# FFN in two phases, gate and up by seven products on two token chunks: a change to a hybrid encoder layer on one Trainium2 core

## The chip, the cores and the metric

The kernel runs on one core of a Trainium2 chip. The core has a matrix engine (TensorE, PE in the profile), a vector engine (VectorE, DVE), a scalar engine (ScalarE, ACT), GpSimd (POOL) and SyncE (SP), which work side by side and wait for each other by semaphores. SP and POOL also hold queues of transfers between DRAM and the on-chip memory. The metric is the device time of one run in microseconds (us).

## The reference

One layer of an encoder works on 1152 tokens (9 tiles of 128, or three chunks of 384) of 1024 features. The change is all in its last part, the FFN, and in the steps around it:

```
h   = x + w_out(sigmoid(gate_a) * (o_att @ w_att_out) + sigmoid(gate_s) * (y_ssd @ w_ssd_out))
hf  = rmsnorm(h, g_ffn)
out = h + (silu(hf @ w_gate) * (hf @ w_up)) @ w_down
y   = rmsnorm(out, g_final)
```

`w_gate` and `w_up` are 1024 x 2816, `w_down` is 2816 x 1024. All is in fp32.

## The kernel before

A product of two fp32 matrices is made of three matmuls. Each operand is split into a high part (a cast on ACT, line 126) and a low part (value minus high part, on DVE, line 127), and the high by high, high by low and low by high products are added in PSUM (`mm3`, lines 150 to 152). Weights come from DRAM in pieces of 512 KB (`wraw`, three buffers), are split into `whi` and `wlo` (three buffers each), and serve PE from there.

The FFN follows `w_out` and its norm. The `w_out` loop adds each product `ps_h` to `h` on DVE (line 897). `norm_T` then makes the normed tiles: a Square with a sum on ACT (line 162), the root on DVE and POOL (lines 119 and 121), the scaling `hn` on DVE (line 164), eight transposes per tile on PE into two banks `ps_T` (line 168), and their split into the chunk's `T_h`. Chunks 0 and 1 are normed within the last quarter of `w_out`, chunk 2 after it.

The FFN loop takes two tiles of 128 features (f) at a time, 11 pairs in all. For each of the two and for each of three token chunks it makes a gate and an up product, 24 matmuls of 384 columns each, then silu by Tanh (line 918) and two DVE operations (lines 919 and 921), and splits the result `a` into `ah` and `al`, which stay on chip. Then the down product of the pair follows: nine token tiles, two halves of 512 output columns, six matmuls into a bank `ps_d`, and one DVE add of that bank into `h` (line 931), 198 adds in the program. When all pairs are done, a tile's `h` is normed (Square on ACT, line 938, root, `yt` on DVE, line 940) and stored.

A scheduler sets the order of each engine's instructions ahead of the run from priorities, and the engines work through their queues in that order. Each queue is served in order, so an instruction that waits holds back all behind it. Transfers are issued by SP in order as well, and a load whose buffer isn't free holds back the loads behind it.

Ahead of `w_out`, the attention output `o_d` is read back from DRAM in five pieces through one buffer `oc` (line 815), split into `ohl` on ACT and DVE, and multiplied (`ps_ao`, from line 834).

Of the kernel before, what the change touches and what calls it, by code (L numbers as in the profile page):

```python
# [15 lines left out]
P = 128  # L16
D = 1024
# [25 lines left out]
def hybrid_layer_kernel(ctx: ExitStack, tc: tile.TileContext, x_prompt, x_sample, cache_k, cache_v,  # L43
# [20 lines left out]
    tpool = ctx.enter_context(tc.tile_pool(name="tpool", bufs=NC))  # L64
# [13 lines left out]
    bias_d = dram.tile([8, CH, 256], F32, name="bias_d")  # L78

# [105 lines left out]
    def run(gen):  # L185
        for _ in gen:
            pass
# [618 lines left out]
    hp = ctx.enter_context(tc.tile_pool(name="hp", bufs=1))  # L806
    with ExitStack() as ph:
        mp = ph.enter_context(tc.tile_pool(name="mp", bufs=1))
        m = mp.tile([P, KT, T], F32, name="m")
        ohl = hp.tile([P, 2, 4, T], F32R, tag="oh", name="ohl")  # L810
        ohi, olo = ohl[:, 0], ohl[:, 1]
        for t0 in range(0, T, 256):
            w = min(256, T - t0)
# [4 lines left out]
            for j in range(4):  # L818
                split(ohi[:, j, t0:t0 + w].rearrange("p (a w) -> p a w", w=qw),
                      olo[:, j, t0:t0 + w].rearrange("p (a w) -> p a w", w=qw), ov[:, :, j, :])  # L820

        for k in range(0, KT, 2):
# [7 lines left out]
            for kk in range(2):  # L830
                for c in range(NC):
# [5 lines left out]
                    mm3(ps[:, :CW], [(hi[:, j, cc], lo[:, j, cc], ohi[:, j, cs], olo[:, j, cs]) for j in range(4)])  # L837
# [33 lines left out]

    with ExitStack() as ph:
        h = hp.tile([P, NT, D], F32, tag="oh", name="h")
        psum_pools(ph, t=5)
        for t in range(NT):
            ld(out=h[:, t, :], in_=xrows(t))
        with ExitStack() as ph2:
            hnp = ph2.enter_context(tc.tile_pool(name="hnp2", bufs=4))
            gB = hnp.tile([P, D], F32, name="gB2", bufs=1)
            ld(out=gB, in_=g_ffn[0].partition_broadcast(P))  # L880
            fT = []
            for q in range(4):
# [7 lines left out]
                for t in range(NT):  # L890
# [5 lines left out]
                    hs = h[:, t, q * 256:(q + 1) * 256]  # L896
                    vec.tensor_tensor(out=hs, in0=ps[:, :256], in1=hs, op=ALU.add)
                    if q == 3 and t in (3, 6):
                        fT.append(norm_T(len(fT), lambda t: h[:, t, :], gB, hnp, "h"))
            fT += [norm_T(c, lambda t: h[:, t, :], gB, hnp, "h") for c in range(len(fT), NC)]  # L900

        with ExitStack() as ph2:
            fp = ph2.enter_context(tc.tile_pool(name="fp", bufs=2))
            for f0 in range(0, NF, 2):
                ah = fp.tile([P, 2, T], F32R, tag="ah", name=f"ah{f0}")
                al = fp.tile([P, 2, T], F32R, tag="al", name=f"al{f0}")
                for ff in range(2):
                    f = f0 + ff
                    gh, gl = wcols(w_gate[0], f * P, P, f"wfg{f}")
                    uh, ul = wcols(w_up[0], f * P, P, f"wfu{f}")  # L910
                    for c in range(NC):
                        cs = slice(c * CW, (c + 1) * CW)
# [89 lines left out]
```

## Time and profile before

| what | before |
|---|---|
| median of three runs | 1833.37 us (1833.11 to 1834.25) |
| the profiled execution | 1832.23 us, span 1830.4 us |
| PE busy | 1809.0 us, 99% |
| DVE busy | 920.9 us, 50% |
| ACT busy | 508.8 us, 28% |
| POOL busy | 113.1 us, 6% |
| DMA | 163.66 MB moved, 89 GB/s over the span |
| share of PE in the chain that ended last | 96% |

The span is the time from the first to the last event of the profiled execution; 1.83 us lie around it. Busy shares are averages over the whole program. Waits of PE are listed apart by what ended them. In the timeline a row's first two numbers are its start and its length in us; matmuls overlap, so the pace is the distance between two starts, not the length. A number in square brackets at the end of a row is the idle time just before it and what ended that.

### The profile page before, as it was taken

What the parts mean: (1) busy time and instruction counts of PE and PEld (TensorE: products, weight loads), DVE (VectorE), ACT (ScalarE), POOL (GpSimd) and SP (SyncE); (2) the same over time, 40 slices, a digit from 0 to 9 for tenths busy, and PEclk for the clock granted to TensorE, in tenths of its full rate; (3) what the DMA queues carried; (4) which work ended last, traced back from release to release, by engine and by line L of the source; (5) the groups of instructions that cost most, each with busy time, mean ns of one, the idle gap of its engine ahead of it and who ended that gap; (6) DMA issues with size and microseconds to landing.
All of it is one profiled execution on the core that took longest, in us unless ns stands there. A gap on an engine that the chain in (4) does not pass through costs nothing.

```text
span 1830.4 us, 26014 instructions
## 1 busy us (share of the span) xinstructions
PE 1809.0 (99%) x10767; PEld 1704.0 (93%) x10767; DVE 920.9 (50%) x1675; ACT 508.8 (28%) x989; POOL 113.1 (6%) x191
## 2 busy tenths in 40 slices
PE   7999999999999999999999999999999999999998
PEld 6998888999999999999999999989989899898997
DVE  5337777454998853533517343343442433424436
ACT  5235555422433323300305111111112111111112
POOL 1010000111121112000001000000000000000001
PEclk9999999999999999999999999999999999999999
DMA  7412212644755435653111111111101111111112
GB/s 217 82 56 66 66 58 70 202 153 132 222 187 180 147 94 184 209 199 98 59 32 47 47 35 35 47 46 47 47 24 47 47 47 47 27 50 40 47 35 103
DMA packets 193841, 163.66 MB, mean 89 GB/s; under 512 B 17507, under 2 KB 178503, under 8 KB 193580
## 3 DMA queue, kind: packets, MB, share of 16 engines
q1 hardware_dynamic: 183308, 128.54, 23.8%
q0 software_dynamic: 10416, 33.47, 4.7%
q8 instruction: 84, 1.38, 0.3%
q14 instruction: 33, 0.27, 0.0%
HBM read 123.21 MB, written 39.69 MB: 89 GB/s over the span
## 4 chain that ended last, share of the span: by engine, by line
PE 96%; DMA 2%; DVE 1%; ACT 1%; issue 0%; SPq 0%; POOL 0%; POOLq 0%; ACTq 0%
PE ps_mm L150 12%; PE ps_mm L152 11%; PE ps_mm L151 11%; PE ps_d L152 5%; PE ps_d L151 5%; PE ps_d L150 5%; PE ps_g L152 5%; PE ps_g L151 5%; PE ps_g L150 5%; PE ps_u L152 5%; PE ps_u L150 5%; PE ps_u L151 5%; PE ps_h L152 2%; PE ps_h L150 2%; PE ps_h L151 2%; DMA yc<-y_d 1%
## 5 line engine op out<-in xcount | busy, mean ns | idle before, releaser
L931 DVE TENSOR_TENSOR h<-ps_d,h 128x512 f32<-128x512 f32 x198 | 135.9, 691 | 121.8 <-PE ps_d L152 121.8
L150 PE MATMUL ps_g<-T_h,wfg_h 128*128 128x384 f32 x528 | 176.6, 334 | 0.0
L152 PE MATMUL ps_g<-T_h,wfg_l 128*128 128x384 f32 x528 | 176.6, 334 | 0.0
L151 PE MATMUL ps_g<-T_h,wfg_h 128*128 128x384 f32 x528 | 176.6, 334 | 0.0
L151 PE MATMUL ps_u<-T_h,wfu_h 128*128 128x384 f32 x528 | 176.4, 334 | 0.0
L152 PE MATMUL ps_u<-T_h,wfu_l 128*128 128x384 f32 x528 | 176.4, 334 | 0.0
L150 PE MATMUL ps_u<-T_h,wfu_h 128*128 128x384 f32 x528 | 176.4, 334 | 0.0
L151 PE MATMUL ps_d<-wd_l,ah 128*128 128x512 f32 x396 | 156.7, 396 | 0.0
L152 PE MATMUL ps_d<-wd_h,al 128*128 128x512 f32 x396 | 156.6, 395 | 0.0
L150 PE MATMUL ps_d<-wd_h,ah 128*128 128x512 f32 x396 | 153.0, 395 | 0.0
L921 DVE SCALAR_TENSOR_TENSOR fa<-ft,ps_u 128x384 f32<-128x384 f32 x66 | 36.6, 555 | 182.2 <-PE ps_u L152 182.2
L150 PE MATMUL ps_mm<-T_x,wx_h 128*128 128x384 f32 x288 | 100.1, 347 | 0.0
L150 PEld LDWEIGHTS ps_g<-T_h,wfg_h 128*128 128x128 f32 x528 | 99.1, 188 | 0.9
L151 PEld LDWEIGHTS ps_g<-T_h,wfg_h 128*128 128x128 f32 x528 | 99.1, 188 | 0.5
L152 PEld LDWEIGHTS ps_g<-T_h,wfg_l 128*128 128x128 f32 x528 | 99.1, 188 | 0.4
L126 ACT ACTIVATE wfu_h<-wfu_r 128x1024 fp32r<-128x1024 f32 x22 | 23.3, 1061 | 273.9 <-PE ps_d L152 240.8
L152 PEld LDWEIGHTS ps_u<-T_h,wfu_l 128*128 128x128 f32 x528 | 99.1, 188 | 0.0
L151 PEld LDWEIGHTS ps_u<-T_h,wfu_h 128*128 128x128 f32 x528 | 99.1, 188 | 0.0
L150 PEld LDWEIGHTS ps_u<-T_h,wfu_h 128*128 128x128 f32 x528 | 99.1, 188 | 0.0
L152 PE MATMUL ps_mm<-T_x,wx_l 128*128 128x384 f32 x288 | 97.4, 338 | 0.0
L151 PE MATMUL ps_mm<-T_x,wx_h 128*128 128x384 f32 x288 | 97.1, 337 | 0.0
L121 POOL TENSOR_TENSOR rs_r<-rs_v,mhalf 128x1 f32<-128x1 f32 x36 | 24.5, 683 | 1124.6 <-DVE rs_v L119 1124.6
(335 smaller groups left out, 4231.3 us busy)
## 6 DMA issues: line engine op xcount, KB each, us to landing
wfg_r<-in_w_gate_dram SPq DMA_DIRECT2D x22, 512.0 KB, 3.7
wfu_r<-in_w_up_dram SPq DMA_DIRECT2D x22, 512.0 KB, 3.9
wd_r<-in_w_down_dram SPq DMA_DIRECT2D x22, 512.0 KB, 4.1
acB<-ac_d SPq DMA_DIRECT2D x9, 1024.0 KB, 6.9
xbc_d<-cv POOLq DMA_DIRECT2D x36, 192.0 KB, 2.1
xb<-xbc_d SPq DMA_DIRECT2D x9, 768.0 KB, 6.1
wx_r<-in_w_in_dram SPq DMA_DIRECT2D x12, 512.0 KB, 4.5
z_d<-z POOLq DMA_DIRECT2D x24, 192.0 KB, 3.4
```

The costliest lines, as they stand in the source:

```text
L121: gps.tensor_tensor(out=r, in0=v, in1=mhalf[:, :n], op=ALU.pow)
L126: act.activation(hi, src, AF.Copy)
L150: pe.matmul(out, ah, bh, start=(i == 0), stop=False)
L151: pe.matmul(out, ah, bl, start=False, stop=False)
L152: pe.matmul(out, al, bh, start=False, stop=(i == n - 1))
L921: vec.scalar_tensor_tensor(out=a, in0=t, scalar=0.5, in1=pu[:, :CW], op0=ALU.mult, op1=ALU.mult)
L931: vec.tensor_tensor(out=h[:, t, hs], in0=ps, in1=h[:, t, hs], op=ALU.add)
```

## The change

The FFN becomes two phases. In the first, all gate and up products are made and `a` is stored to a DRAM tensor `a_d`, by a queue of POOL. In the second, the down product reads `a` and `w_down`, and adds over all 22 feature tiles in PSUM, so that nothing is added on DVE but once per bank at the end.

Gate and up on chunks 0 and 1 use a form with seven products for two by two blocks. The blocks are the two halves of the 1024 input features, the two feature tiles of a pair, and the two chunks. Each product is 12 matmuls of 384 columns (4 slices x 3). Sums of weight blocks (S1 to S4) are made on DVE in `prep`, sums of the activations (T1 to T4) once in `combine`, from raw fp32 copies of the transposed tiles. Products that share a destination are added in PSUM (banks `ps_a`, `ps_b`, `ps_c`), the rest by five DVE adds of 128x384 in `tail`. Chunk 2 goes by the plain form (`plain`, bank `ps_c2`).

In the second phase the token tiles go in two groups, of 5 and of 4, each through two halves of output columns, so `w_down` is read twice. `h` is stored to DRAM in the norm and read back as `y` in the second phase. At the end the last three pairs of the last half are run tile by tile. `o_d` is read in six pieces (256 and 128 columns of each chunk) rather than five.

On PE, at the end of `w_out`. `ps_h` is the product of `w_out`, `ps_T` the transposes, `hn_h` a normed tile (before, `hn_h_9733` and `hn_h_9755` are tiles 6 and 7; after, the three are tiles 6, 7 and 8), `ps_g` or `ps_a` the first gate product. Before:

```order
L151 MATMUL ps_h<-wo_l,T_m_8578 128x256
L152 MATMUL ps_h<-wo_h,T_m_8578 128x256
L168 MATMUL ps_T<-cp,hn_h_9733 128x128 x8
L150 MATMUL ps_g<-T_h_9468,wfg_h 128x384
L151 MATMUL ps_g<-T_h_9468,wfg_h 128x384
L152 MATMUL ps_g<-T_h_9468,wfg_l 128x384
```

Before, 40 gate and up matmuls further on:

```order
L152 MATMUL ps_u<-T_h_9468,wfu_l 128x384
L150 MATMUL ps_u<-T_h_9468,wfu_h 128x384
L168 MATMUL ps_T<-cp,hn_h_9755 128x128 x8
L151 MATMUL ps_u<-T_h_9468,wfu_h 128x384
L152 MATMUL ps_u<-T_h_9468,wfu_l 128x384
```

After:

```order
L155 MATMUL ps_h<-wo_h,T_m_8592 128x256
L913 MATMUL ps_T<-cp,hn_h_9765 128x128 x8
L913 MATMUL ps_T<-cp,hn_h_9788 128x128 x8
L913 MATMUL ps_T<-cp,hn_h_9811 128x128 x8
L881 MATMUL ps_a<-T_h_9489,wfg_h 128x384
L882 MATMUL ps_a<-T_h_9489,wfg_h 128x384
```

The transposes of the last two tiles moved from among the first gate and up matmuls to ahead of all of them.

On DVE at the same place. Before, from the last add of `ps_h` (`hn_h_9755` and `hn_h_9777` are tiles 7 and 8):

```order
L897 TENSOR_TENSOR h<-ps_h,h 128x256
L119 TENSOR_SCALAR rs_v<-ss 128x1
L127 TENSOR_TENSOR wfg_l<-wfg_r,wfg_h 128x1024
L164 SCALAR_TENSOR_TENSOR hn_h_9755<-h,rs_r,gB_8612 128x1024
L127 TENSOR_TENSOR T_h_9732<-ps_T,T_h_9732 128x4x128 x2
L119 TENSOR_SCALAR rs_v<-ss 128x1
L919 SCALAR_TENSOR_TENSOR ft<-ft,ps_g 128x384
L164 SCALAR_TENSOR_TENSOR hn_h_9777<-h,rs_r,gB_8612 128x1024
```

After, from the last add of `ps_h` (`raw` are the fp32 copies, `T_X` holds T1 and T2):

```order
L951 TENSOR_TENSOR h_8612<-ps_h,h_8612 128x256
L925 TENSOR_TENSOR raw_8633<-raw_8634,raw_8633 128x1536
L908 SCALAR_TENSOR_TENSOR hn_h_9788<-h_8612,rs_r,gB_8631 128x1024
L130 TENSOR_TENSOR wfu_l<-wfu_r,wfu_h 128x1024
L925 TENSOR_TENSOR raw_8634<-raw_8634 128x1536
L122 TENSOR_SCALAR rs_v<-ss 128x1
L130 TENSOR_TENSOR T_X<-raw_8633,T_X 128x1536
L130 TENSOR_TENSOR T_h_9764<-ps_T,T_h_9764 128x4x128 x4
L908 SCALAR_TENSOR_TENSOR hn_h_9811<-h_8612,rs_r,gB_8631 128x1024
```

Three operations of `combine` now stand between the last add and the norm of the last tile, and four splits of transposed tiles.

On ACT, where the first phase ends (`wd_0_4_h` is the high part of the third piece of `w_down`, whose buffer the last weights of up hold until the last but one matmul of the phase; `a_0` is the first piece of `a` read back, which the first down matmul needs). After:

```order
L1060 ACTIVATE fsg<-ps_c_13782 128x384
L1024 ACTIVATE p_13823<-ps_a 128x384
L129 ACTIVATE wd_0_2_h<-wd_0_2_r 128x1024
L129 ACTIVATE wd_0_4_h<-wd_0_4_r 128x1024
L129 ACTIVATE a_0_13988<-ar_0_14010 128x1280
L129 ACTIVATE a_2_13989<-ar_2_14050 128x1280
```

Before there is no such place: `a` is split from where DVE left it, pair by pair, and no load stands in front of it.

The diff, cut to its core (`prep`, `plain` and the views of arrays are left out where the words above say the same):

```diff
-        ohl = hp.tile([P, 2, 4, T], F32R, tag="oh", name="ohl")
-        for t0 in range(0, T, 256):
-            w = min(256, T - t0)
+        ohl = [hp.tile([P, 2, 4, CW], F32R, tag="oh", name=f"ohl{c}") for c in range(NC)]
+        for t0, w in ((c * CW + o, w) for c in range(NC) for o, w in ((0, 256), (256, 128))):
...
+            def combine(T1, T2, T3, T4):
+                b11, b21 = raws[0][:, :4, :], raws[0][:, 4:, :]
+                b12, b22 = raws[1][:, :4, :], raws[1][:, 4:, :]
+                sub = lambda out, a, b: vec.tensor_tensor(out=out, in0=a, in1=b, op=ALU.subtract)
+                sub(b11, b12, b11)
+                split(T1[:, 0], T1[:, 1], b11)
+                yield
+                sub(b11, b22, b11)
+                split(T2[:, 0], T2[:, 1], b11)
+                sub(b12, b22, b12)
+                split(T3[:, 0], T3[:, 1], b12)
+                sub(b21, b21, b11)
+                split(T4[:, 0], T4[:, 1], b21)
...
+            parts = combine(T1, T2, T3, T4)
+            next(parts)
+            tls[2] = tpool.tile([P, 2, KT, CW], F32R, tag="T", name="T_h2")
+            norm2(2)
+            run(parts)
...
+            def head(w, use):
+                a = bank("t", "ps_a")[:, :CW]
+                mma(a, terms(w["A11"], B11), True, False)
+                p1 = st_("p1")
+                act.activation(p1, a, AF.Copy)
+                mma(a, terms(w["A12"], B21), False, True)
+                use(0, 0, a)
+                return p1
...
+            def tail(w, use, p1):
+                b, c = bank("t", "ps_b")[:, :CW], bank("t", "ps_c")[:, :CW]
+                add = lambda out, ps, x: vec.tensor_tensor(out=out, in0=ps, in1=x, op=ALU.add)
+                u2, u3 = st_("u2"), st_("u3")
+                mma(b, terms(w["S2"], T2), True, False)
+                add(u2, b, p1)
+                mma(c, terms(w["S1"], T1), True, False)
+                mma(b, terms(w["S3"], T3), False, False)
+                add(u3, b, p1)
+                add(u3, c, u3)
+                use(1, 1, u3)
+                mma(c, terms(w["S4"], B22), False, True)
+                add(u2, c, u2)
+                use(0, 1, u2)
+                mma(b, terms(w["A22"], T4), False, True)
+                add(p1, b, p1)
+                use(1, 0, p1)
...
-                        ps = bank("t", "ps_d")
-                        mm3(ps, [(ah[:, ff, tk], al[:, ff, tk], wd[ff][0][:, hs], wd[ff][1][:, hs]) for ff in range(2)])
-                        vec.tensor_tensor(out=h[:, t, hs], in0=ps, in1=h[:, t, hs], op=ALU.add)
...
+        for t0, n in ((0, 5), (5, 4)):
...
+            for dh in range(2):
+                hs = slice(dh * 512, (dh + 1) * 512)
+                pss = [bank("t", "ps_d") for _ in range(n)]
...
+                for f0 in range(0, NF, 2):
+                    w = wload([(view, w_down[0, f0 * P:(f0 + 2) * P, hs].rearrange("(k p) c -> p k c", p=P))],
+                              1024, f"wd{t0}_{dh}_{f0}")
...
+                            ld(out=ar, in_=a_d[f0 * P:(f0 + 2) * P, t0 * P:(t0 + n) * P]
+                               .rearrange("(k p) t -> p k t", p=P))
+                            split(at[f0][:, 0], at[f0][:, 1], ar)
```

## Rows read from the trace of the kernel before

**Rows 1.** Page, busy time of each engine, share of the span, instructions

```profile
PE 1809.0 (99%) x10767; PEld 1704.0 (93%) x10767; DVE 920.9 (50%) x1675; ACT 508.8 (28%) x989; POOL 113.1 (6%) x191
```

**Rows 2.** Waits of PE, whole span: total us, times, longest

```profile
PE ps_T L168 <- DVE hn_x L164: 9.7, 2, 8.5
...
PE ps_ao L150 <- ACT gs L629: 0.9, 1, 0.9
```

**Rows 3.** Windows: us, busy (instructions) of each engine, PE clock, DMA share, GB/s

```profile
1005.00:1820.00 815.00, 815.00 (x4295) 761.47 (x4294) 322.48 (x470) 136.20 (x210) 3.70 (x7) 1.00 0.14 43
```

**Rows 4.** Timeline of PE, gate matmuls, start and length in us

```profile
1072.89 0.33 PE L150 MATMUL ps_g<-T_h,wfg_h 128*128 128x384 f32 x1
...
1074.97 0.33 PE L150 MATMUL ps_u<-T_h,wfu_h 128*128 128x384 f32 x1
```

**Rows 5.** Chain of waits, FFN, the down product's rows of two pairs

```profile
1046.44 0.47 PE ps_d L150 x2
...
1121.59 0.47 PE ps_d L150 x2
```

**Rows 6.** Groups of DVE and ACT, 700 to 1831: busy, mean ns, idle before

```profile
L931 DVE TENSOR_TENSOR h<-ps_d,h 128x512 f32<-128x512 f32 x198 | 135.9, 691 | 121.8 <-PE ps_d L152 121.8
L127 DVE TENSOR_TENSOR wfg_l<-wfg_r,wfg_h 128x1024 fp32r<-128x1024 f32 x22 | 26.9, 1222 | 4.0 <-ACT wfg_h L126 4.0
L897 DVE TENSOR_TENSOR h<-ps_h,h 128x256 f32<-128x256 f32 x36 | 15.2, 423 | 53.3 <-PE ps_h L152 53.3
L127 DVE TENSOR_TENSOR T_h<-ps_T,T_h 128x512 fp32r<-128x512 f32 x18 | 11.7, 685 | 3.5 <-ACT T_h L126 3.5
L164 DVE SCALAR_TENSOR_TENSOR hn_h<-h,rs_r,gB 128x1024 f32<-128x1024 f32 x9 | 11.5, 1282 | 2.3 <-POOL rs_r L121 2.2
...
L126 ACT ACTIVATE wd_h<-wd_r 128x1024 fp32r<-128x1024 f32 x22 | 23.4, 1062 | 61.5 <-PE ps_g L151 31.6 <-issue 27.2 <-PE ps_u L151 2.7
```

**Rows 7.** Timeline of PE, end of w_out and first gate/up matmuls

```profile
993.02 1.04 PE L168 MATMUL ps_T<-cp,hn_h 128*128 128x128 f32 x8
993.81 0.43 PE L150 MATMUL ps_g<-T_h,wfg_h 128*128 128x384 f32 x1
...
1000.84 1.04 PE L168 MATMUL ps_T<-cp,hn_h 128*128 128x128 f32 x8
```

**Rows 8.** Chain of waits, the end

```profile
1822.24 0.25 PE ps_d L152
...
1823.30 1.06 ACT yt L938
```

**Rows 9.** Windows at the end (columns as in rows 3)

```profile
1822.00:1824.00 2.00, 0.47 (x3) 0.04 (x1) 1.75 (x4) 0.70 (x1) 0.55 (x1) 1.00 0.66 262
1824.00:1826.00 2.00, 0.00 (x0) 0.00 (x0) 1.19 (x3) 0.45 (x2) 0.55 (x1) 0.68 0.39 158
1826.00:1828.00 2.00, 0.00 (x0) 0.00 (x0) 0.64 (x1) 0.00 (x0) 0.00 (x0) 0.50 0.53 213
```

**Rows 10.** Timeline of PE, the start of the program

```profile
8.46 1.97 PE L168 MATMUL ps_T<-cp,hn_x 128*128 128x128 f32 x8 [8.46 <-DVE hn_x L164]
...
17.96 0.67 PE L150 MATMUL ps_mm<-T_x,wk_h 128*128 128x384 f32 x1
...
19.96 0.34 PE L151 MATMUL ps_mm<-T_x,wv_h 128*128 128x384 f32 x1
```

**Rows 11.** Chain of waits and timeline of PE at the attention output

```profile
729.40 2.77 DMA oc<-o_d
...
734.99 0.45 PE L150 MATMUL ps_ao<-ohl,wa_h 128*128 128x384 f32 x1 [0.92 <-ACT gs L629]
```

**Rows 12.** Page, DMA issues (KB each, us to landing); window at the start

```profile
wd_r<-in_w_down_dram SPq DMA_DIRECT2D x22, 512.0 KB, 4.1
...
8.00:10.00 2.00, 1.54 (x7) 1.54 (x8) 0.56 (x2) 1.54 (x3) 0.28 (x1) 1.00 1.03 420
```

More of the change, by code (lines that the diff above doesn't have):

```diff
@@ L78, in hybrid_layer_kernel @@
     bias_d = dram.tile([8, CH, 256], F32, name="bias_d")
+    h_d = dram.tile([T, D], F32, name="h_d")
+    a_d = dram.tile([FF, T], F32, name="a_d")
     banks = {}
@@ L836, in hybrid_layer_kernel @@
                     cc = slice(kk * P, (kk + 1) * P)
[L837 removed]
+                    mm3(ps[:, :CW], [(hi[:, j, cc], lo[:, j, cc], ohl[c][:, 0, j, :], ohl[c][:, 1, j, :]) for j in range(4)])
                     vec.scalar_tensor_tensor(out=m[:, k + kk, cs], in0=gt, scalar=1.0, in1=ps[:, :CW],
@@ L869, in hybrid_layer_kernel, with mma @@
             mT.append(tl)
+    def mma(ps, terms, start, stop):
+        n = len(terms)
+        for i, (ah, al, bh, bl) in enumerate(terms):
+            pe.matmul(ps, ah, bh, start=start and i == 0, stop=False, skip_group_check=True)
+            pe.matmul(ps, ah, bl, start=False, stop=False, skip_group_check=True)
+            pe.matmul(ps, al, bh, start=False, stop=stop and i == n - 1, skip_group_check=True)
     with ExitStack() as ph:
-        h = hp.tile([P, NT, D], F32, tag="oh", name="h")
+        h = [hp.tile([P, 3, D], F32, tag="oh", name=f"h{c}") for c in range(NC)]
@@ new lines, in hybrid_layer_kernel, with norm2 @@
+            tls = {}
+            def norm2(c):
+                if c == 0:
+                    tls[c] = tpool.tile([P, 2, KT, CW], F32R, tag="T", name=f"T_h{c}")
+                for tt in range(3):
+                    t = 3 * c + tt
+                    ht = h[c][:, tt, :]
+                    hn = hnp.tile([P, D], F32, tag="hn", name=f"hn_h{t}")
+                    ss = sm.tile([P, 1], F32, tag="ss", name="ss")
+                    act.activation(hn, ht, AF.Square, accum_out=ss)
+                    r = rstd_of(ss, 1)
+                    vec.scalar_tensor_tensor(out=hn, in0=ht, scalar=r, in1=gB, op0=ALU.mult, op1=ALU.mult)
+                    st(out=h_d[t * P:(t + 1) * P, :], in_=ht)
+                    for k0 in range(0, KT, 4):
+                        ps = bank("t", "ps_T")
+                        for k in range(4):
+                            pe.transpose(ps[:, k * P:(k + 1) * P], hn[:, (k0 + k) * P:(k0 + k + 1) * P], ident)
+                        pv = ps.rearrange("p (k t) -> p k t", k=4)
+                        kk, tk = slice(k0, k0 + 4), slice(tt * P, (tt + 1) * P)
+                        if c != 1:
+                            split(tls[c][:, 0, kk, tk], tls[c][:, 1, kk, tk], pv)
+                        if c < 2:
+                            act.activation(raws[c][:, kk, tk], pv, AF.Copy)
@@ new lines, in hybrid_layer_kernel @@
+                        norm2(t // 3 - 1)
+            tX = tpool.tile([P, 2, 2, 4, CW], F32R, tag="T", name="T_X")
+            T1, T2 = tX[:, 0], tX[:, 1]
+            T3, T4 = (hp.tile([P, 2, 4, CW], F32R, tag="oh", name=f"T_Y{i}") for i in range(2))
+            parts = combine(T1, T2, T3, T4)
[3 more added lines that the diff above has]
+            run(parts)
+            B22 = hp.tile([P, 2, 4, CW], F32R, tag="oh", name="T_Y2")
```

187 lines of the change are left out of this document (142 added, 45 removed).

## The prediction

> **What bounds the kernel now.** I read the page's busy line first, then PE's waits, then PE's rows in the FFN. PE is busy 1809.0 of 1830.4 us [rows 1]; its waits are 9.7 us at the program's start and 0.9 us around 735, plus two smaller ones [rows 2]; from 1005 to 1820 it is busy in every microsecond at a granted clock of 1.00, with DVE at 322 of 815 us and ACT at 136 [rows 3]. So TensorE alone sets the FFN's time, and what counts is how many matmuls are issued, and whether anything makes PE wait that doesn't now. The two matmuls of 384 columns shown stand twelve starts apart, with no gap between: (1074.97 - 1072.89) / 12 = 0.1733 us each [rows 4]; two of 512 columns take 0.47 us, so about 0.234 each [rows 5]. A pair of feature tiles is 288 x 0.1733 + 108 x 0.234 = 75.2 us, and the down product's row of one pair comes back after 1121.59 - 1046.44 = 75.15 us [rows 5]. The count explains the time.
>
> **Matmuls taken away.** Before, gate or up of one pair is 2 tiles x 3 chunks x 24 = 144 matmuls. After, chunks 0 and 1 take seven products of 12 = 84 instead of 96, chunk 2 keeps 48: 132. There are 22 such units: 22 x 12 = 264 fewer, at 0.1733 us 45.8 us. The down product keeps its 1188 matmuls of 512 columns; accumulating in PSUM over all features only changes their order. So **-45.8 us**, and this term has no freedom as long as PE stays full.
>
> **Vector work.** The 198 adds of ps_d into h go (135.9 us [rows 6]), and so do the splits of `a` per chunk. They lay beside PE, so taking them away is worth nothing. New on DVE in a unit: four sums of 128x512 (0.69 each, the T_h row of that shape), four splits of 128x1024 (1.22), five tail adds and six gate or up operations of 128x384 (under 0.69 each): 2.8 + 4.9 + at most 7.6, 15.3 us at most against 132 x 0.1733 = 22.9 us of PE [rows 6]. PE's order puts 24 or 25 matmuls (4.2 us) between a product that DVE must read out and the next one that writes the same bank, so an add of 0.69 us with one 1.22 us split ahead of it is hidden. I cost it at 0; if one more split and one sum stood ahead each time it would still fit; the cover is gone when the add comes more than 4.2 us late.
>
> **The entry to the FFN.** Before, the last ps_h is followed by the eight transposes of tile 6, then by gate matmuls of chunk 0 at once, and the transposes of tile 7 come 7 us later, between matmuls [rows 7], those of tile 8 in the same way. After, all 24 transposes of chunk 2 stand ahead of the first ps_a (the order above). The last eight need hn of tile 8, and on DVE that stands behind: the last h add 0.42, three 128x1536 operations (estimate from 0.685 at 512 and 1.222 at 1024: 1.76 each), hn of tile 7 1.28, a weight split 1.22, four T_h splits 0.685 and itself 1.28 [rows 6]: 0.42 + 5.28 + 1.28 + 1.22 + 2.74 + 1.28, and 0.15 for a short one, makes 12.4 us after the last ps_h. Eight transposes follow at 0.8 to 0.9 (993.02 to 993.81, and the matmul behind them 0.1 us slower) [rows 7], so the first ps_a starts at 13.3; 24 transposes are 2.6 us of work that before has as well. PE idles **+10.7 us**. The low end is 8 (neighbouring DVE operations start before the one before has ended, about 0.1 us each, and the scheduler's DVE gaps may be filled otherwise), the high end 14 (each wait across ACT and POOL in that chain pays up to a few tenths, and the ACT splits may come late).
>
> **The clock after that hole.** At the end of the program the last matmul ends at 1822.49 [rows 8]; the granted clock of the stretch 1822 to 1824 is still 1.00, that of 1824 to 1826 is 0.68 and then 0.50, the 1.2 GHz level [rows 9]. The new hole has a stretch of some 7 us with no PE work between tile 7's and tile 8's transposes, so the clock will have fallen. At the start of the program, after 8.46 us of idling, eight transposes took 1.97 us instead of 0.88, and matmuls that begin at 17.96 run at full pace by 19.96 [rows 10]. So the last transposes cost 1.1 us more and the matmuls behind them about 1 us: **+2 us**. The bounds are 0 and 5 (half pace over the 10 us that the start shows). The Trainium skill, TensorE: Matmul & The Clock Gate, says in Part 4 that transposes do not count as PE work for the clock as matmuls do, and its table in "Why this matters for your kernels" warns of idle gaps between bursts of matmuls. By that the change has made a cold start where before had none, and the whole entry, transposes included, would run at the low clock, at the 5 us end; the start's rows agree that transposes alone didn't raise the pace, but show the matmuls back at full pace soon, so I stay at 2.
>
> **From gate/up to down.** The first ps_d matmul waits for the split of a0 on ACT, and ACT's queue has wd_0_4_h ahead of it, which can only start when the last but one gate/up matmul frees its buffer. That is 1.06 us [rows 6] and then 128x1280 at 1.06 x 1.25 = 1.33: **+2.4 us** of PE idle. The second step's low half on DVE comes at about 3.8 us + its 1.5, ten matmuls (2.3 us) behind: hidden or nearly. Bounds 1 and 6. The clock held through 1.5 us of idling at the end [rows 9], so I add nothing for it here.
>
> **Smaller edits.** The attention output's reload goes from five pieces of o_d to six through one buffer. PE waited 0.92 us there already, and the last small piece took 2.77 us to land [rows 11], so one more piece is 0 to 3.7 us with its splits: **+1.5**. At the end the Square is over half a row (1.06 us becomes about 0.6 [rows 8]) with a short add: **-0.3**. The h rows now go out to DRAM and come back, and `a` too; these transfers ride on the POOL and SP queues. The a_d stores of all but the last unit are long done when the down phase starts; h is needed only after 77 us of down.
>
> **Sum.** -45.8 + 10.7 + 2 + 2.4 + 1.5 - 0.3 = -29.5. Against the profiled execution, 1832.23 (span 1830.4 and 1.83 around it), 1802.7. The median of the runs is 1.1 us above that execution, so I say **1803.5**.
>
> **Rivals.** (a) *The entry is hidden.* If DVE clears its queue faster than its order suggests, or matmuls get ahead, only 2 to 4 us of stalls stay: about 1790. Against it: PE's queue is in order and the first ps_a stands behind the last transposes. Chance 0.12. (b) *Many small hand-overs.* Each of the 22 units loses some 0.5 us, because an add reaches its turn on DVE behind a split that itself waits for ACT and a weight load: 22 x 0.5 = +11, about 1815. For it: three engines and a load in one chain; against it: 4.2 us of cover and DVE under 70% busy. Chance 0.15. (c) *Slower than before: the first pass of down waits for its loads.* Each step of the first half loads 512 KB of w_down and 640 KB (later 512 KB) of `a` from DRAM. One transfer at a time, 512 KB take 4.1 us [rows 12], so a step costs 9.2 us (8.2) where PE works 30 x 0.234 = 7.0 us (24: 5.6). Over eleven steps each that is +24 and +29 us: 1803.5 + 53 = 1856. It decides from 29.5/22 = 1.3 us per step. For it: `ar` has two buffers, one queue issues both, and a load that waits for a split holds the next ones back. Against it: at 8 to 10 us the engines moved 420 GB/s [rows 12], three times the 164 GB/s that a step needs, so transfers do overlap. Chance 0.05, and 0.05 for a part of it that ends between 1815 and 1832. (d) *The hole costs more* (high ends: 14 us idle, 5 for the clock, 6 at the boundary): about 1814, inside my own range. (e) *The change doesn't do what it says:* the count of matmuls in its program is 264 fewer; no chance given.
>
> **How the numbers follow.** The forecast with its bounds (1796 to 1814) has 0.63, (a) 0.12, (b) 0.15, the partial (c) 0.05, the whole (c) 0.05. The range 1790 to 1820 leaves out the top of (b) and all of (c) and the lower half of (a): under 0.2. About 0.2% (3.7 us) is what a measurement of this kernel tells from no change. Faster 0.92, same 0.02, slower 0.06.
>
> **What would show it.** In the profile after: 0.173 us between gate/up matmuls and 22.9 us from unit to unit; a PE wait on ps_T for hn of DVE near 993 that sums to 8 to 14 us, with a granted clock under 1.00 in that stretch; a wait of 1 to 6 us ahead of the first ps_d, released by ACT; no waits of ps_b or ps_c for DVE; ps_d matmuls 0.234 us apart with no DMA wait. Waits on `ar` or w_down in the first pass would make it (c), ps_b or ps_c waits (b). I am wrong in kind if the FFN's matmuls are issued at another pace than before.

## The result and the profile after

The changed kernel takes 1801.85 us (median of four runs, 1801.27 to 1803.15), the kernel before 1833.24 us (four runs). The ratio is 0.983, with a 95% interval of 0.981 to 0.985: 31 us less, where 1803.5 us were forecast in a range of 1790 to 1820. The profiled execution has a span of 1800.2 us, 30.2 us under the span of before.

The page's busy line of the kernel after, and its waits of PE (total us, times, longest), which answer to [rows 1] and [rows 2]:

```profile
PE 1765.7 (98%) x10503; PEld 1666.3 (93%) x10503; DVE 986.5 (55%) x1731; ACT 592.7 (33%) x1066; POOL 158.7 (9%) x266
```

```profile
PE ps_T L913 <- DVE hn_h L908: 8.8, 2, 6.2
PE ps_ao L153 <- ACT gs L632: 3.4, 2, 3.1
```

PE's list has 264 matmuls fewer (10767 to 10503). Within the units and within the down phase PE waits for nothing (no ps_b, ps_c, ps_c2, no load): what stands between the products of the seven-product form is long enough for DVE, and the two passes over w_down are fed in time. The new waits are at three places, all on the list of the prediction: the entry (8.8 us), the attention output (3.4 us where it was 0.9), and the change of phase (2.1 us, shown below).

The entry on PE (timeline, start and length in us, idle before). The first row follows the last ps_h without a gap:

```profile
996.46 1.03 PE L913 MATMUL ps_T<-cp,hn_h 128*128 128x128 f32 x8
1000.09 1.94 PE L913 MATMUL ps_T<-cp,hn_h 128*128 128x128 f32 x8 [2.60 <-DVE hn_h L908]
1008.21 1.94 PE L913 MATMUL ps_T<-cp,hn_h 128*128 128x128 f32 x8 [6.18 <-DVE hn_h L908]
1009.81 0.67 PE L881 MATMUL ps_a<-T_h,wfg_h 128*128 128x384 f32 x1
...
1010.91 0.52 PE L881 MATMUL ps_a<-T_h,wfg_h 128*128 128x384 f32 x1
1011.24 0.52 PE L882 MATMUL ps_a<-T_h,wfg_h 128*128 128x384 f32 x1
```

DVE in the same stretch, the queue that the last hn stands in:

```profile
998.67 1.28 DVE L908 SCALAR_TENSOR_TENSOR hn_h<-h,rs_r,gB 128x1024 f32<-128x1024 f32 x1
...
1002.73 1.75 DVE L130 TENSOR_TENSOR T_X<-raw,T_X 128x1536 fp32r<-128x1536 f32 x1
1004.40 2.48 DVE L130 TENSOR_TENSOR T_h<-ps_T,T_h 128x512 fp32r<-128x512 f32 x4
1006.79 1.27 DVE L908 SCALAR_TENSOR_TENSOR hn_h<-h,rs_r,gB 128x1024 f32<-128x1024 f32 x1
```

It is the forecast queue, in the order that stands ahead of the prediction, and the 1536-wide operations take 1.75 us for the estimated 1.76. The last transposes begin 11.75 us after the first ones.

The windows of that stretch (us, then busy time and instructions of PE, PEld, DVE, ACT and POOL, PE clock, DMA share, GB/s); DVE is busy in all of it:

```profile
998.00:1000.00 2.00, 0.00 (x0) 0.00 (x0) 2.00 (x3) 2.00 (x4) 0.00 (x0) 0.91 0.66 262
1000.00:1002.00 2.00, 1.91 (x8) 1.57 (x8) 2.00 (x2) 2.00 (x4) 0.00 (x0) 0.50 0.00 0
...
1010.00:1014.00 4.00, 4.00 (x16) 4.00 (x16) 4.00 (x4) 2.31 (x3) 0.00 (x0) 0.59 0.00 0
```

The granted clock falls to 0.50, the 1.2 GHz level, towards the end of the first hole, which is 2.6 us long (0.91 in the window 998 to 1000), and is back only within the last of these windows. Until then the 384-column matmuls stand up to 0.33 us apart (1010.91 to 1011.24) rather than 0.173.

The change of phase on PE, from the first ps_d matmul on, and two windows:

```profile
1521.22 0.50 PE L881 MATMUL ps_d<-wd_h,a 128*128 128x512 f32 x1 [2.13 <-ACT a L129]
...
1522.58 0.63 PE L881 MATMUL ps_d<-wd_h,a 128*128 128x512 f32 x1
1523.01 0.63 PE L882 MATMUL ps_d<-wd_l,a 128*128 128x512 f32 x1
```

```profile
1520.00:1522.00 2.00, 0.78 (x3) 0.68 (x4) 1.96 (x2) 2.00 (x3) 0.54 (x1) 0.97 0.79 162
1522.00:1524.00 2.00, 2.00 (x6) 1.54 (x6) 2.00 (x2) 0.34 (x1) 0.00 (x0) 0.50 0.99 278
```

Here the clock fell behind 2.1 us of idling, and it fell when PE, which starts at 1521.22, was at work again (0.97 in the window up to 1522, then 0.50): the ps_d matmuls behind that stand 0.43 us apart (1522.58 to 1523.01).

Two paces were not forecast. The down matmuls, from the chain of waits (fourteen starts from one to the other, 0.226 us each, where the prediction read 0.234 from [rows 5] and the runs below give 0.2333):

```profile
1784.96 0.23 PE ps_d L883
...
1788.13 0.24 PE ps_d L883
```

And a product with a sum of weight blocks, from the timeline of PE (twelve starts apart, 2.12 / 12 = 0.1767 us, where [rows 4] has 0.1733):

```profile
1204.42 0.34 PE L881 MATMUL ps_b<-T_Y,wfg8s_h 128*128 128x384 f32 x1
...
1206.54 0.33 PE L881 MATMUL ps_c<-T_h,wfg_h 128*128 128x384 f32 x1
```

All starts of PE's rows, taken against these paces (0.2333 and 0.2267 us for down, 0.1733 and 0.1767 for the sums), give the account of the 30.2 us:

| term | forecast | from the two traces |
|---|---|---|
| 264 matmuls fewer | -45.8 | -45.8 |
| entry, idle | +10.7 | +8.8 |
| entry, low clock | +2 | +4.0 |
| change of phase, idle | +2.4 | +2.3 |
| change of phase, low clock | 0 | +1.7 |
| up to the last ps_h (of it attention output +3.1) | +1.5 | +3.4 |
| end | -0.3 | -0.2 |
| pace of down, 1188 x 6.7 ns | 0 | -7.9 |
| pace of the sums, 1056 x 3.4 ns | 0 | +3.6 |
| sum | -29.5 | -30.1 |

### The profile page after: what moved, and what is told of

Read it like the earlier page. It is cut to its first block, busy times and chain, and to the rows that moved or that the text cites. A ratio compares the mean times of both kernels' runs of the same rounds, so it can differ in the third digit from the quotient of the medians.

```text
span 1800.2 us, 26065 instructions
## 1 busy us (share of the span) xinstructions
PE 1765.7 (98%) x10503; PEld 1666.3 (93%) x10503; DVE 986.5 (55%) x1731; ACT 592.7 (33%) x1066; POOL 158.7 (9%) x266
## 4 chain that ended last, share of the span: by engine, by line
PE 92%; DMA 3%; DVE 2%; issue 1%; ACT 1%; POOL 0%; SPq 0%; POOLq 0%; ACTq 0%; DVEq 0%
PE ps_mm L153 11%; PE ps_mm L155 11%; PE ps_mm L154 11%; PE ps_c L881 5%; PE ps_c L882 5%; PE ps_c L883 5%; PE ps_d L881 5%; PE ps_d L882 5%; PE ps_d L883 5%; PE ps_b L883 3%; PE ps_b L882 3%; PE ps_b L881 3%; PE ps_h L154 2%; PE ps_h L155 2%; PE ps_h L153 2%; PE ps_a L881 2%
## 5 line engine op out<-in xcount | busy, mean ns | idle before, releaser
L881 PE MATMUL ps_d<-wd_h,a 128*128 128x512 f32 x396 | 154.7, 392 | 2.1 <-ACT a L129 2.1
L882 PE MATMUL ps_d<-wd_l,a 128*128 128x512 f32 x396 | 155.0, 392 | 0.0
L883 PE MATMUL ps_d<-wd_h,a 128*128 128x512 f32 x396 | 153.3, 389 | 0.0
L881 PEld LDWEIGHTS ps_d<-wd_h,a 128*128 128x128 f32 x396 | 74.9, 189 | 18.1 <-ACT a L129 2.4
L882 PEld LDWEIGHTS ps_d<-wd_l,a 128*128 128x128 f32 x396 | 74.9, 189 | 15.4
L883 PEld LDWEIGHTS ps_d<-wd_h,a 128*128 128x128 f32 x396 | 74.5, 188 | 15.6
L154 PE MATMUL ps_h<-wo_l,T_m 128*128 128x256 f32 x288 | 81.5, 284 | 0.0
L155 PE MATMUL ps_h<-wo_h,T_m 128*128 128x256 f32 x288 | 81.5, 283 | 0.0
L153 PE MATMUL ps_h<-wo_h,T_m 128*128 128x256 f32 x288 | 81.1, 283 | 0.0
L153 PE MATMUL ps_mm<-T_x,wga_h 128*128 128x384 f32 x192 | 65.9, 343 | 0.0
L155 PE MATMUL ps_mm<-T_x,wz_l 128*128 128x384 f32 x192 | 65.2, 340 | 0.0
L153 PE MATMUL ps_mm<-T_x,wz_h 128*128 128x384 f32 x192 | 64.9, 338 | 0.0
L155 PE MATMUL ps_mm<-T_x,wga_l 128*128 128x384 f32 x192 | 64.9, 338 | 0.0
L154 PE MATMUL ps_mm<-T_x,wz_h 128*128 128x384 f32 x192 | 64.8, 338 | 0.0
```

What stands on the lines that cost most here:

```text
L153: pe.matmul(out, ah, bh, start=(i == 0), stop=False)
L154: pe.matmul(out, ah, bl, start=False, stop=False)
L155: pe.matmul(out, al, bh, start=False, stop=(i == n - 1))
L881: pe.matmul(ps, ah, bh, start=start and i == 0, stop=False, skip_group_check=True)
L882: pe.matmul(ps, ah, bl, start=False, stop=False, skip_group_check=True)
L883: pe.matmul(ps, al, bh, start=False, stop=stop and i == n - 1, skip_group_check=True)
```

## The experiments

Runs of one kernel lie up to 6 us apart here (1794.0 to 1799.8 us in x3b_norm_forced). What an edit of a few us is worth is therefore read from the starts of PE's matmuls in the profiled run too, in three stretches: up to the last ps_h, from there to the last gate or up matmul, and from there to the last ps_d. The table of them stands at the end of this section.

**Without the seven-product form (x5_plain).** All three chunks go by the plain form, in the same two phases; the sums are gone.

```diff
-                cl = tls[2]
-                for i in range(2):
+                for j in range(3):
+                    cl = tls[j]
+                    for i in range(2):
...
-            parts = combine(T1, T2, T3, T4)
```

> The changed kernel without the seven-product form: two phases, all three chunks by the plain form, no sums of weights or activations. Theory, nearly all of the gain is the 264 matmuls: 45.8 us more for them, 3.6 us less for the pace of the sums, some 6 us less at the entry where combine is gone, 1838 us (1832 to 1843), that is no faster than before. Rival, the two phases with PSUM accumulation carry a good part of the gain by themselves: 1810 to 1825 us.

Measured: 1831.5 us against 1833.5 of before, ratio 0.9989 (0.9980 to 0.9998). The two phases alone are worth 2 us, and only because down runs at 0.2267 us in this kernel too, which is 7.9 us that the next experiment puts down to addresses; without that they would have cost some 6 us (the difference of the two). The seven-product form brings the rest, 29.7 us; the terms that go with it in the account (-45.8, +12.8 for the entry, +3.6 for the sums) make 29.4. The rival is out. The entry has no hole here:

```profile
996.07 0.34 PE L881 MATMUL ps_c<-T_h,wfg_h 128*128 128x384 f32 x1
996.24 1.03 PE L912 MATMUL ps_T<-cp,hn_h 128*128 128x128 f32 x8
```

Matmuls of chunk 0 stand between the transposes, as in the kernel before. So the whole entry cost (12.8 us) belongs to the seven-product form as it is written, not to the two phases. The 1831.5 lie below the forecast 1838 because that one took only 6 of these 12.8 us away.

**The pace of down (x1_before_pad, x1b_before_pad224).** Both are the kernel before, with a few unused bytes per partition ahead of the pool of `ah` and `al`:

```diff
+            pad = ph2.enter_context(tc.tile_pool(name="pad", bufs=1)).tile([P, 8], F32, name="pad")
+            vec.memset(pad, 0.0)
             fp = ph2.enter_context(tc.tile_pool(name="fp", bufs=2))
```

The second has 56 words for the 8. In the memory plans of the two programs, `ah` and `al` alone lie elsewhere, 192 bytes further.

> The kernel before, with 32 bytes per partition put ahead of the pool of ah and al, so that these stationary operands of the down product start 32 bytes later (at 32 instead of 0 modulo 64, as the split a does in the changed kernel). Theory A, the address of the stationary operand sets the pace: the 1188 down matmuls go from 0.2333 to 0.2267 us, 7.9 us less, about 1825.3 us. Theory B, the pace comes from accumulating over all features in PSUM or from the missing adds on DVE: 0.2333 us stays, 1833 us.

> The kernel before again, now with 224 bytes ahead of the pool of ah and al, so that they start at 96 modulo 128 and at 224 modulo 256, as the weights, the transposed activations and the split a of the changed kernel do (32 bytes put them at 32 modulo 128). Theory A, in a new form: the pace is full where the stationary operand starts like that: 0.2333 goes to 0.2267 us, about 1825.5 us. Theory B, as before: 0.2333 stays, 1833 us.

With 32 bytes: 1833.7 us, ratio 1.0004 (0.9994 to 1.0013), no change. With 224 bytes: 1826.5 us, ratio 0.9963 (0.9951 to 0.9975), 7 us less. The chain of waits at the end of each, ps_d matmuls twelve starts apart, first with 32 bytes, then with 224:

```profile
1818.00 0.23 PE ps_d L150
...
1820.80 0.23 PE ps_d L150
```

```profile
1813.16 0.23 PE ps_d L150
...
1815.88 0.23 PE ps_d L150
```

2.80 / 12 = 0.2333 and 2.72 / 12 = 0.2267 us. The only difference is 192 bytes in the start of the stationary operands, so their place alone makes the whole step, in a kernel that has neither the accumulation over all features nor the adds taken off DVE. That the changed kernel owes its pace to the same is shown by x6_shift below, where it loses it by a shift. Theory B is out, and the first form of theory A (32 modulo 64) as well.

**The pace of the sums (x2_sums_pad).** The same 32 bytes ahead of the pool of the sums `sp`; nothing but the sums moves.

> The changed kernel, with 32 bytes per partition put ahead of the pool that holds the sums of weight blocks, so that these stationary operands start at 32 instead of 0 modulo 64, like the other weights. Theory A: the 1056 matmuls with a sum go from 0.1767 to 0.1733 us, 3.6 us less, about 1798 us. Theory B, their layout (four blocks side by side) or the change of banks sets it: 0.1767 stays, 1802 us.

Measured: 1799.3 us, ratio to before 0.9811 (0.9796 to 0.9825), 2.6 us under the changed kernel; from the last ps_h to the last gate or up matmul it takes 4.5 us less (the pace gives 3.6 of them), and up to the last ps_h it took 2.1 us more. The timeline of PE, a product with sums, eleven starts apart, 1.91 / 11 = 0.174 us:

```profile
1204.59 0.33 PE L881 MATMUL ps_b<-T_Y,wfg8s_h 128*128 128x384 f32 x1
...
1206.50 0.33 PE L883 MATMUL ps_b<-T_Y,wfg8s_l 128*128 128x384 f32 x1
```

The same columns in the same layout at 0.1733 us instead of 0.1767; theory B is out here too.

**All weights shifted (x6_shift).** 32 bytes near the bottom of the memory move every weight to 0 modulo 128 bytes; the activations and the split `a` stay at 96.

> The changed kernel with 32 bytes added near the bottom, so that all weights start at 0 modulo 128 instead of 96, while the activations and the split a stay at 96 and the sums come to 96. Theory A (the stationary operand's own start): products with plain weights go from 0.1733 to 0.177 to 0.180 us, those with sums to 0.1733, down (moving operand shifted, stationary not) stays at 0.2267. Theory A2 (both operands must start alike): the same for gate and up, but down goes to 0.2333. Theory B: no pace changes.

Measured: 1806.3 us (one run). The ps_d matmuls in the chain of waits, twelve starts apart:

```profile
1793.23 0.23 PE ps_d L883
...
1796.03 0.23 PE ps_d L883
```

2.80 / 12 = 0.2333: down is slow again, this time with its moving operand shifted and its stationary one unshifted. But the gate and up products with plain weights kept 0.1733, with the stationary operand at 0, and `w_out`, whose moving operand is shifted like that of down, got faster. Timeline of PE, two up matmuls and then two of `w_out`, each pair twelve starts apart, 2.08 / 12 = 0.1733 and 1.40 / 12 = 0.1167 us:

```profile
1099.94 0.34 PE L884 MATMUL ps_c<-T_h,wfu_h 128*128 128x384 f32 x1
...
1102.02 0.34 PE L884 MATMUL ps_c<-T_h,wfu_h 128*128 128x384 f32 x1
```

```profile
893.10 0.28 PE L157 MATMUL ps_h<-wo_h,T_m 128*128 128x256 f32 x1
...
894.50 0.28 PE L157 MATMUL ps_h<-wo_h,T_m 128*128 128x256 f32 x1
```

In the changed kernel twelve starts of `w_out` take 1.44 us, 0.1200 each. From its first to its last matmul `w_out` takes 106.0 us here and 108.7 there. All pairs that the runs have (starts modulo 128 bytes by the memory plans, paces by the traces):

| columns | product | stationary at | moving at | us each | run |
|---|---|---|---|---|---|
| 512 | down | 0 | 96 | 0.2333 | before |
| 512 | down | 32 | 96 | 0.2333 | x1_before_pad |
| 512 | down | 96 | 96 | 0.2267 | after, x1b_before_pad224 |
| 512 | down | 96 | 0 | 0.2333 | x6_shift |
| 384 | gate, up | 96 | 96 | 0.1733 | before, after |
| 384 | gate, up | 0 | 96 | 0.1733 | x6_shift |
| 384 | sums | 64 | 96 | 0.1767 | after |
| 384 | sums | 96 | 96 | 0.1733 | x2_sums_pad |
| 256 | `w_out` | 96 | 96 | 0.1200 | after |
| 256 | `w_out` | 96 | 0 | 0.1167 | x6_shift |

So it is neither the stationary start alone (A) nor a rule that both must start alike (A2), and each theory missed a part of this run. Where both start at 96, 384 and 512 columns had the best pace seen, but 256 columns did not: the pair 96 and 0 is the slower one for 512 and the faster one for 256. Which rule lies behind stays open.

**The entry: order on DVE (x3_norm_first, x3b_norm_forced).** The first writes `norm2(2)` ahead of `combine`:

```diff
-            parts = combine(T1, T2, T3, T4)
-            next(parts)
             tls[2] = tpool.tile([P, 2, KT, CW], F32R, tag="T", name="T_h2")
             norm2(2)
-            run(parts)
...
+            parts = combine(T1, T2, T3, T4)
+            run(parts)
```

> The changed kernel, with the norm of chunk 2 written ahead of all of combine, so that no sum over the raw copies stands ahead of the last hn on DVE. Theory: the entry's 8.8 us of idle PE come from that queue; they fall to 2 to 5 us, the clock has less of a hole to fall in, and the time falls by 5 to 10 us to about 1794 us. Rival, the hole has other causes (the root on POOL, the Square on ACT, weight splits) or the sums then come too late for the first tail: no change, 1800 to 1803 us.

Measured: 1803.9 us, and PE's wait for hn_h is 8.8 us as before the edit. DVE's order came out as before the edit, with a 1536-wide operation of combine again between the last add and the norm of tile 7 (without it, in the next run, DVE waits 0.4 us there for the root on POOL). So this run says nothing on the theory. The second, in the same written order, ties combine to the last norm:

```diff
+                    if t == NT - 1:
+                        for rw in (raws[0], raws[1]):
+                            vec.scalar_tensor_tensor(out=rw[:, 0, :1], in0=hn[:, :1], scalar=0.0,
+                                                     in1=rw[:, 0, :1], op0=ALU.mult, op1=ALU.add)
```

> The changed kernel with combine made to wait for the norm of the last tile (two operations on one column per partition, which add zero times hn of that tile to the raw copies, tie it), since written order alone left the three operations of combine ahead of it on DVE. Theory: without these 5.3 us and two of the four T_h splits the last transposes start at about 1001.5 after a ps_h end at 996.5, where they started at 1008.2: 6 to 7 us less idle and 1 to 2 us less at the low clock, about 1794 us. Rival, the sums' late end stalls the first tail, or another chain takes the place: 1799 to 1803 us.

Measured: 1795.3 us, ratio 0.9798 (0.9780 to 0.9816), 6.6 us under the changed kernel. Timeline of PE:

```profile
997.55 1.06 PE L917 MATMUL ps_T<-cp,hn_h 128*128 128x128 f32 x8 [1.43 <-ACT T_h L129]
1001.73 1.94 PE L917 MATMUL ps_T<-cp,hn_h 128*128 128x128 f32 x8 [3.12 <-DVE hn_h L908]
...
1004.65 0.34 PE L882 MATMUL ps_a<-T_h,wfg_h 128*128 128x384 f32 x1
1004.82 0.34 PE L883 MATMUL ps_a<-T_h,wfg_l 128*128 128x384 f32 x1
```

The last transposes begin at 1001.73, as expected, the idle time falls from 8.8 to 4.6 us, and the matmuls have full pace from 1004.65, after a few slow ones. The operations of combine in DVE's queue are shown as the cause of that part of the hole. A wait of 0.8 us of ps_c behind a gate operation is new. By the starts the edit is worth 5.0 us, with that wait. Another 1.7 us of this run are not the edit's: PE idles the same 2.13 us at the change of phase, but the clock didn't fall there (1.00 in the window 1515 to 1517).

**The entry: the bank (x11_head_bank).** `ps_a` of the first two units comes from the other pool of PSUM banks; nothing else changes.

```diff
-                a = bank("t", "ps_a")[:, :CW]
+                a = (mmt("ps_a") if first[0] else bank("t", "ps_a"))[:, :CW]
```

> The changed kernel, with ps_a of the first two units taken from the other pool of PSUM banks, which ps_T doesn't use; DVE's order stays as it is. In PE's order the 24 matmuls of the two first ps_a now stand between the transposes of tiles 6, 7 and 8 instead of behind them. Theory: it was the bank that ps_a shares with ps_T that put the matmuls behind the transposes; 24 x 0.173 = 4.2 us of the 8.8 us idle time are filled, and the stretch at the low clock is shorter: 4 to 6 us less, about 1796.5 us. Rival: the matmuls run in the hole at half pace and the transposes of tile 7 come later, so that DVE's queue ends later too: under 2 us less.

The 24 matmuls did move between the transposes. Measured: 1798.8 us, ratio 0.9802 (0.9786 to 0.9818), 3 us less by the medians, and 1.4 us less by the starts up to the last gate or up matmul; here too the clock didn't fall at the change of phase (1.00 in the window 1523 to 1525), which is 1.6 us more and not the edit's. So the theory's 4 to 6 us did not come, and its rival (under 2 us) has the size. PE:

```profile
1000.10 0.42 PE L881 MATMUL ps_a<-T_h,wfg_h 128*128 128x384 f32 x1
...
1011.06 1.94 PE L913 MATMUL ps_T<-cp,hn_h 128*128 128x128 f32 x8 [3.66 <-DVE hn_h L908]
```

So the place of the matmuls behind the transposes in PE's order was a matter of the banks that they share, which I had not seen. But with DVE's queue as it is, filling the hole gives little: the last transposes come 11.75 us after the first all the same (999.31 to 1011.06), and the clock is low later, when PE has work (384-column matmuls 0.32 us apart up to 1019.9).

**Is it the clock? (x7_fill_hole)** Five fp32 products of no use stand between the transposes of tiles 7 and 8.

```diff
+                    if t == NT - 1:
+                        fill = mmt("ps_fill")
+                        for i in range(5):
+                            pe.matmul(fill[:, :CW], ident, prev[0][:, :CW], start=True, stop=True)
```

> The changed kernel with work of no use in the hole of the entry: five fp32 products of a normed tile with the identity, 384 columns each, between the transposes of tiles 7 and 8 (the result is not used). DVE's queue is as it was, so the last transposes can start no earlier. Theory: what is slow behind the hole (transposes at 0.2 us each, ps_a at 0.32 us) is the clock that fell in it; with PE at work the ps_a matmuls start at 0.173 us, and 1.5 to 2.6 us come back. Rival, they are slow for another reason (their operands or banks): they stay at 0.32 us.

Measured: 1803.2 us (one run), no gain in the time; by the starts behind the last ps_h it is 0.8 us, under the 1.5 to 2.6 expected. The first ps_a matmuls in the timeline, and the windows:

```profile
1011.37 0.34 PE L882 MATMUL ps_a<-T_h,wfg_h 128*128 128x384 f32 x1
1011.54 0.48 PE L883 MATMUL ps_a<-T_h,wfg_l 128*128 128x384 f32 x1
1011.82 0.52 PE L881 MATMUL ps_a<-T_h,wfg_h 128*128 128x384 f32 x1
1012.14 0.52 PE L882 MATMUL ps_a<-T_h,wfg_h 128*128 128x384 f32 x1
```

```profile
1008.00:1010.00 2.00, 0.00 (x0) 0.00 (x0) 2.00 (x3) 0.00 (x0) 0.00 (x0) 1.00 0.00 0
...
1012.00:1014.00 2.00, 2.00 (x8) 2.00 (x7) 2.00 (x2) 0.46 (x2) 0.00 (x0) 0.50 0.04 8
```

The first matmuls start 0.17 us apart, then, on the same tiles and the same bank, 0.32: the granted clock went from 1.00 to 0.50 between them. So what is slow behind the hole is the clock, and operands and banks are out. But most of the gain failed: the clock stayed up through the filled hole (and through the 2.6 us ahead of it, where it fell in the changed kernel), and it fell behind the 3.8 us of idling that were left after the fill, once PE was at work again. Filling half of the hole moved the low clock to the matmuls behind it.

**The change of phase (x4_pool_hi).** The high part of the third piece of w_down is made on POOL:

```diff
-        act.activation(hi, src, AF.Copy)
+        if pool:
+            gps.tensor_copy(out=hi, in_=src)
+        else:
+            act.activation(hi, src, AF.Copy)
```

> The changed kernel, with the high part of the third piece of w_down made on POOL instead of ACT, so that ACT's queue has nothing ahead of the split of a0 that waits for the last up matmuls. Theory: the 2.1 us wait of PE ahead of the first ps_d falls under 0.7 us and the ps_d matmuls behind it run at 0.227 us at once (no 1.7 us at the low clock), 3 to 4 us less, about 1798 us. Rival, another split or load is late next: the wait stays above 1.5 us.

Measured: 1800.5 us (one run). The timeline of PE:

```profile
1521.24 0.50 PE L884 MATMUL ps_d<-wd_h,a 128*128 128x512 f32 x1
1521.58 0.39 PE L885 MATMUL ps_d<-wd_l,a 128*128 128x512 f32 x1
1521.80 0.39 PE L884 MATMUL ps_d<-wd_h,a 128*128 128x512 f32 x1
```

No wait stands before the first row (PE's excess there falls from 2.3 to 0.3 us), and the next ones are 0.22 us apart: idle time and low clock are both gone, 3.6 us by the starts. The single time shows less, since this run had lost 1.8 us more than the changed kernel ahead of the FFN; the local reading is the one to trust.

**The attention output (x8_five_pieces).** `o_d` in five pieces again, the second of them split into two chunks' tiles.

```diff
-        for t0, w in ((c * CW + o, w) for c in range(NC) for o, w in ((0, 256), (256, 128))):
+        for t0 in range(0, T, 256):
+            w = min(256, T - t0)
```

> The changed kernel with o_d read back in five pieces as before, the second of them split into two chunks' tiles. Theory: the sixth reload of the one buffer caused the longer wait at 735 to 738; PE's wait for ps_ao by ACT falls from 3.4 to about 1 us, 2 to 3 us less, about 1799 us. Rival: the wait comes from the order on ACT and stays at 3 to 4 us.

Measured: 1800.0 us (one run). The wait of PE:

```profile
PE ps_ao L153 <- ACT gs L632: 1.4, 1, 1.4
```

It falls from 3.4 to 1.4 us. The whole stretch, from the first to the last ps_ao matmul on PE, takes 54.1 us before (729.75 to 783.81), 57.1 in the changed kernel (730.46 to 787.58) and 54.0 here (732.13 to 786.15). So the sixth reload is all of the 3.1 us that this part lost. The single time shows only 1.8 us less because this run came to the stretch 1.7 us later.

The reload can cost more than that. In the changed kernel's profile the clock stays up behind the wait of 3.1 us; in the eight other profiles with six pieces it falls to 0.50 in or just behind the waits there. First the changed kernel, then x2_sums_pad:

```profile
738.00:740.00 2.00, 1.53 (x9) 1.54 (x10) 1.93 (x3) 1.43 (x4) 0.54 (x1) 1.00 0.22 75
```

```profile
742.00:744.00 2.00, 2.00 (x8) 2.00 (x8) 1.29 (x3) 0.00 (x0) 0.00 (x0) 0.50 0.83 214
```

**All of it together (x12_all).** Sums at their new place, combine behind the last norm, the bank, the split on POOL, five pieces.

> All edits together: sums at 32 modulo 64, combine behind the last norm, ps_a of the first two units in the other banks, the high part of the third piece of w_down on POOL, o_d in five pieces. If their gains add up: 3.6 (sums) + 6.5 (norm order) + 4 (bank; less than alone, since the hole is smaller) + 3.7 (boundary) + 2 (pieces) = 20 us less than the changed kernel, about 1782 us. Rival: the holes overlap or move into a new wait at the first tail or in front of ps_d: 1787 to 1792 us.

Measured: 1793.0 us (four runs), ratio to before 0.9773 (0.9759 to 0.9788), the fastest of all and 9 us under the changed kernel, but 11 us over the sum. Timeline of PE, then of DVE:

```profile
1020.20 0.69 PE L889 MATMUL ps_a<-T_h,wfu_h 128*128 128x384 f32 x1 [7.52 <-DVE fsg L1076]
```

```profile
1015.05 3.42 DVE L133 TENSOR_TENSOR T_Y<-raw,T_Y 128x1536 fp32r<-128x1536 f32 x2
...
1019.61 0.54 DVE L1076 SCALAR_TENSOR_TENSOR fsg<-fsg,ps_a 128x384 f32<-128x384 f32 x1
```

The rival was right in kind, and just above its 1787 to 1792. The combine that is now behind the norm stands in front of the first gate operation on DVE, and that one frees the bank that the second unit's ps_a now needs, since it moved to the small pool. The hole of the entry is closed but for 2 us in small waits, and another of 7.5 us opens ten microseconds later, with its own stretch at the low clock. The other three edits kept what they had given: 3.6 us at the change of phase, 3.0 in the attention output (54.2 us), of which a start 1.0 us later in this run hides a part, and 3.6 for the sums. From the last ps_h to the last gate or up matmul the run gains only 3.8 us, so the two edits of the entry together brought next to nothing. A version that moves only the first unit's ps_a would test this reading; it was not run.

The three stretches (us, from the starts of PE's matmuls in each profiled run):

| run | up to the last ps_h | to the last gate or up | to the last ps_d |
|---|---|---|---|
| after | 996.3 | 522.4 | 273.3 |
| x2_sums_pad | 998.5 | 518.0 | 273.3 |
| x3b_norm_forced | 995.0 | 517.4 | 271.6 |
| x11_head_bank | 999.2 | 521.0 | 271.7 |
| x7_fill_hole | 998.4 | 521.6 | 273.3 |
| x4_pool_hi | 998.1 | 522.7 | 269.7 |
| x8_five_pieces | 995.0 | 521.8 | 273.2 |
| x12_all | 994.4 | 518.6 | 269.7 |

## Why the prediction was right

*The matmuls.* The count gave -45.8 us, and it is there: PE stayed full through all units, and the kernel without the seven-product form is 29.7 us slower, which is this count less the form's own costs.

*No freedom in this term.* This step failed. I held that the down product in PSUM "only changes their order", and that PE staying full was all that the term needed. The pace of a matmul was taken as given by its columns, but the split `a` and the sums came to lie at other addresses: -7.9 us on down and +3.6 us on the sums. "I am wrong in kind if the FFN's matmuls are issued at another pace than before", says the prediction, and they were. The net of -4.3 us was luck, and it covered the terms that came out too small: 1.7 us of clock at the change of phase and 1.9 us up to the last ps_h.

*DVE and ACT at nothing.* Right. No wait of PE within the units, with DVE at 55% of the span. Rival (b), 0.5 us lost in each unit, has no row.

*The entry.* The mechanism, its place and its queue were right, and 12.8 us against the forecast 12.7 nearly the size. The split between the two terms was off, and that the errors cancel is luck: 8.8 us idle (10.7 forecast; DVE's queue was some 0.8 us shorter, as neighbours there overlap by 0.1 us each, and tile 7's transposes, 0.9 us longer than at full pace, took up time that had been counted as idle) and 4.0 us of low clock (2 forecast). The clock fell in the first hole of 2.6 us and not only in the long one, so both sets of transposes were slow. That is nearer to the bound of 5 us, a low clock in the whole entry, than to the 2. The Trainium skill, TensorE: Matmul & The Clock Gate, says in Part 4 that transposes don't count as PE work like matmuls, and warns in its table in "Why this matters for your kernels" of idle gaps between bursts. Here tile 7's transposes, alone between two holes, did not bring the clock back (0.50 in their window), which agrees, though the holes around them could do it alone. Against rival (a), the entry hidden: in x11_head_bank matmuls do stand between the transposes; in the changed kernel the shared banks forbade it.

*The change of phase.* The idle time was right (2.1 to 2.3 us for 2.4). That the clock would hold, read from 1.5 us of idling at the end [rows 9], failed: behind 2.1 us it fell, for 1.7 us more. The same rows held the warning: 0.68 over 1824 to 1826 is what comes out if the clock falls from 1.00 to 0.50 at about 1824.7 (an estimate), 2.2 us after the last matmul, and the forecast wait was 2.4. Taking wd_0_4_h out of ACT's queue removed both. In two of the experiments the clock held through the same 2.13 us, so the 1.7 us are not certain either.

*The attention output.* The mechanism was right and the size too small: the sixth reload cost 3.1 us for the forecast 1.5, and five pieces bring them back. Of the 3.4 us up to the last ps_h, 0.7 are a later start of this stretch, where other runs of the same code lie up to 2.3 us later still, and what follows it is 0.3 us shorter.

*The slow rival.* Loads one at a time, 1856 us: no row of PE waits for `ar`, `w_down` or `y`. The transfers overlap: 278 GB/s in the window 1522 to 1524, where 512 KB in the 3.7 us from issue to landing, one at a time, would be 142.

## What to carry over

When a form with fewer products is put in, count the matmuls first, and then look at the one place where its operands are made: here the steady part gave all that the count promised, and over a quarter of it was lost again in the 13 us of the entry, where the sums are built and PE has little to do. A short hole can cost more than its length, since the clock may fall in it or just behind it, so what is ahead of the first dependent matmul in a vector engine's queue is worth ordering by dependency and not by the order of the text, and the order on all engines has to be looked at again after each such edit. And a matmul's pace is to be read from starts in the trace for each pair of operands, before the term "count times pace" is called certain. An edit of a few us is read from the stretch that it touches, since the clock at other places can differ from one run to the next by as much.

## What the runs showed of the hardware

The start address of a matmul's operands within a partition changes its pace, with nothing else changed: 0.2333 or 0.2267 us for 512 columns (x1_before_pad against x1b_before_pad224, 7 us of the kernel), and 0.1767 or 0.1733 us for 384 (the changed kernel against x2_sums_pad). With both operands at 96 modulo 128 bytes these two widths had the best pace seen, but 256 columns were faster with the moving operand at 0 (0.1167 against 0.1200 us, x6_shift). The rule behind it is open.

The granted clock can fall late: in x7_fill_hole and at the change of phase it went to 0.50 after PE had taken up work again. And the length of a hole did not decide alone. Behind the 2.13 us at the change of phase the clock fell in the changed kernel and held in x3b_norm_forced and x11_head_bank; behind the 3.1 us at the attention output it held in the changed kernel (1.00 in the window 738 to 740) and fell behind a like one of 3.0 us in x2_sums_pad (0.50 at 742 to 744). What decided is not shown.
